# Attention scores on TensorE: one stacked query against paired key parts

## The chip, the cores and the metric

The kernel runs on one core of a Trainium2 chip. A core has five engines with a queue each: TensorE (PE in the profile; PEld is its weight load), VectorE (DVE), ScalarE (ACT), GpSimd (POOL) and SyncE (SP), which issues most DMAs here. Engines wait for each other through semaphores. The time is microseconds on the device for one execution. A matmul takes a stationary operand (loaded as weights, up to 128x128) and streams a moving operand of up to 512 columns past it; its result goes to PSUM, which DVE and ACT read.

## What is computed

The reference is one decoder block for 1024 positions and 1024 channels: a combined input projection, a spatial gating branch, a dilated window attention branch, a merge, and a convolutional MLP. The change is in the attention scores. There are three head groups with 4 heads of 64 dims each; a group with dilation `dil` splits the sequence into `dil` residues, and in each residue blocks of 128 queries see their own 128 keys and the 128 before them:

```python
DILATED_GROUPS = ((128, 1), (512, 4), (2048, 16))
def banded_window_attention(q, k, v, steps):
    ...
    qb = blocks(q)
    kc = with_prev(blocks(k))
    vc = with_prev(blocks(v))
    scores = jnp.einsum('nbqhd,nbkhd->nbhqk', qb, kc, ...) * (HEAD_DIM ** -0.5)
    ...
    band = (dist >= 0) & (dist <= steps)
    first_ok = (jnp.arange(nb)[:, None, None] > 0) | (ki[None] >= ATTN_BLOCK)
    scores = jnp.where(valid[None, :, None], scores, -jnp.inf)
    m = jnp.max(scores, axis=-1, keepdims=True)
    p = jnp.exp(scores - m)
    den = jnp.sum(p, axis=-1, keepdims=True)
    out = jnp.einsum('nbhqk,nbkhd->nbqhd', (p / den).astype(v.dtype), vc)
```

Everything is float32. The first block of a residue has no block before it, so it sees its own keys alone.

## The kernel before

**Numbers in two parts.** A float32 matmul would be slow on PE, so operands are split into a high part (rounded to `float32r`) and a low part (the rest, also `float32r`), and products are made of part products. `to_parts` makes them: ACT copies with rounding, DVE subtracts.

**Stages.** The input projection runs first, as 27 pairs of 128-column weight tiles; each pair is made by 7 products (a Strassen-like scheme, `in_product`, line 544), and each product is 12 matmuls of 128x512. From the pairs of group 1 on (order of the groups: 1, 2, 0), attention is woven into this stream. After every 6 projection matmuls `tick()` counts a clock on, and work that was put off with `after(lag, fn)` for that count is written out. So the order on PE is fixed by the program; on DVE, ACT, POOL and SP the order after the first 18 products is chosen by the framework's own planner when the program is built, and each engine then runs its queue strictly in that order.

**One block of attention** (class `Attend`, 24 of them: 8 for each group, `T` = 0 to 7) is started at tick `s` after its group's values are there: `load` brings the block's 64-dim queries and keys from DRAM, each twice, one copy in partitions 0 to 63 and one in 64 to 127 (line 840, SP; 3 buffers); `turn` at `s` makes the parts; `score` at `s+3` makes the scores (lines 865, 866), their maximum (line 879, DVE), and the exponentials (line 893, ACT, after the negated maximum on DVE, line 891); `turn_p` at `s+8` transposes them on PE (line 904) and copies the transposes out (910 ACT, 912 DVE); `product` at `s+10` multiplies by the values (line 920). Blocks start 5 ticks apart, so several are under way at once.

**The parts of a block.** `kk`, in a ring of 3 slots (`kring`), holds the keys' high part in partitions 0 to 63 and the low part in 64 to 127. `qa` and `qb` hold the high and the low part of the queries, each in both halves. A matmul of 128 partitions with `qa` thus sums query-high times key-high and query-high times key-low, and one with `qb` adds the two terms with query-low. So each head takes two matmuls of 256 columns, 8 per block.

**With and without a block before.** In group 0 blocks 1 to 7 have a block before them, in group 1 the odd ones, in group 2 none: 11 blocks have one, 13 have none. For the 11 the 256 columns are two ring slots. For the 13 the same 128 keys are streamed twice (a broadcast), and only columns 128 to 255 are used.

**Group 0** also mixes the three groups (`combine`, called in `product`): SP loads the stored results of groups 1 and 2 (line 939, tiles `ld`), DVE makes weights from them (lines 948 to 959), POOL applies them (971, 972). The first of these DVE instructions, `nmin` (line 948), waits for the loads; a load waits until POOL has finished with the same buffer one block earlier.

Of the kernel before, what the change touches and what calls it, by code (L numbers as in the profile page):

```python
# [12 lines left out]
F32R = mybir.dt.float32r  # L13
BF16 = mybir.dt.bfloat16
I32 = mybir.dt.int32
AF = mybir.ActivationFunctionType
ALU = mybir.AluOpType
# [3 lines left out]
P = 128  # L21
# [7 lines left out]
NH = 4  # L29
# [7 lines left out]
GROUPS = (1, 2, 0)  # L37
FIRST = 2
UW = NH * HD + 2 * NH
KSLOTS = 3  # L40

INV_FREQ = [float(np.float32(500000.0 ** (-i / ROT))) for i in range(0, ROT, 2)]

# [51 lines left out]
def block_kernel(  # L95
# [61 lines left out]
    def f32(ap):  # L157
        return ap.bitcast(F32)
# [654 lines left out]
    class Attend:  # L813
# [28 lines left out]
            self.q_raw, self.k_raw = got  # L842

        def turn(self):
            qa = at.tile([P, NH, P], F32R, name=f"qa_{self.name}", tag="qa", bufs=1)
            qb = at.tile([P, NH, P], F32R, name=f"qb_{self.name}", tag="qb", bufs=1)
            kk = kring[:, self.slot]
            nc.scalar.activation(kk, self.k_raw, AF.Copy)
            nc.vector.tensor_tensor(
                kk[64:P], self.k_raw[64:P], f32(kk[64:P]), ALU.subtract  # L850
            )
            to_parts(qa, qb, self.q_raw, nc.vector)
            self.qa, self.qb = qa, qb

        def score(self):
            name = self.name
            sc = ps_x.tile([P, 2, 2, 256], F32, name=f"sc_{name}", tag="sc")
            s0, s1 = (t % KSLOTS for t in self.halves)
            for h in range(NH):
                if self.has_prev:  # L860
                    keys = kring[:, s0 : s1 + 1 : s1 - s0, h, :]
                else:
                    keys = kring[:, s0, h, :].unsqueeze(1).to_broadcast([P, 2, P])
                dst = sc[:, h % 2, h // 2, :]
                nc.tensor.matmul(dst, self.qa[:, h, :], keys, start=True, stop=False)  # L865
                nc.tensor.matmul(dst, self.qb[:, h, :], keys, start=False, stop=True)  # L866
            lo = 0 if self.has_prev else P
            st = at.tile([P, UW], F32, name=f"st_{name}", tag="st", bufs=2)
            mx = small.tile([P, NH], F32, name=f"mx_{name}", tag="mx")
            pr_t = at.tile([P, NH, 256], F32, name=f"pr_{name}", tag="pr", bufs=2)  # L870
            if self.g == 2:
                mk = mask2
            elif self.has_prev:
                o = 0 if self.halves[0] < self.T else P
                mk = mask[:, o : o + 256]
            else:
                mk = mask[:, P : 2 * P]
            for h in range(NH):
                nc.vector.tensor_tensor_reduce(
                    out=pr_t[:, h, lo:256],  # L880
                    in0=sc[:, h % 2, h // 2, lo:256],
                    in1=mk,
                    op0=ALU.add,
                    op1=ALU.max,
                    scale=1.0,
                    scalar=-3.0e38,
                    accum_out=mx[:, h : h + 1],
                )
            nm = st[:, 256 : 256 + NH]
            den = st[:, 256 + NH : 256 + 2 * NH]  # L890
            nc.vector.tensor_scalar(nm, mx, -0.125, None, ALU.mult)
            for h in range(NH):
                nc.scalar.activation(
                    pr_t[:, h, lo:256], pr_t[:, h, lo:256], AF.Exp,
                    bias=nm[:, h : h + 1], scale=0.125, accum_out=den[:, h : h + 1],
                )
            self.st, self.pr = st, pr_t
# [115 lines left out]
    def open_attention():  # L1013


        nonlocal at, kring, mask, mask2
        at = at_stack.enter_context(tc.tile_pool(name="at", bufs=2, reuse_waits="tile"))
        kring = at.tile([P, KSLOTS, NH, P], F32R, name="kring", bufs=1)
        mask = at.tile([P, 3 * P], F32, name="mask", bufs=1)
        mask2 = at.tile([P, P], F32, name="mask2", bufs=1)  # L1020
        sign = at.tile([P, 256], F32, name="sign", tag="vt", bufs=8)[0:1, 0:P]
        nc.gpsimd.memset(mask, 0.0)
        nc.gpsimd.memset(sign[:, 0::2], 1.0)
        nc.gpsimd.memset(sign[:, 1::2], -1.0)
        for m in (mask[:, 0:P], mask[:, 2 * P : 3 * P]):
            nc.gpsimd.affine_select(
                out=m, in_=m, compare_op=ALU.is_ge, fill=NEG,
                base=0, pattern=[[1, P]], channel_multiplier=-1,
            )

        def causal(m):
            nc.gpsimd.affine_select(
                out=m, in_=m, compare_op=ALU.is_ge, fill=NEG,
                base=0, pattern=[[-1, P]], channel_multiplier=1,
            )

        def parity_mask():
            pg = tr_tile("pg")
            nc.tensor.matmul(pg[:, :P], sign, sign, start=True, stop=True)
            nc.vector.tensor_scalar(mask2, pg[:, :P], 1.0, -0.5 * NEG, ALU.subtract, ALU.mult)  # L1040
            causal(mask2)

        causal(mask[:, P : 2 * P])
        after(8, parity_mask)
# [1463 lines left out]
```

## Time and profile before

| what | value |
|---|---|
| three runs | 1362.97, 1362.97, 1362.02 us (median 1362.97) |
| the profiled execution's own time | 1362.35 us |
| its span in the profile | 1360.6 us (1.75 us lie around it) |
| granted TensorE clock | 0.998 |
| PE / DVE / ACT / POOL busy over the span | 1352.0 / 1030.4 / 642.0 / 313.5 us |
| score matmuls (lines 865, 866) | 192, from 157.4 to 391.6 us |
| stretch with attention in it, 150 to 401 us | PE 251.0 of 251 us busy, DVE 193.0, ACT 142.1 |

Rows of the timeline start with the start in us and the duration in us; then engine, line, operation, output <- input, how many were merged, and in brackets how long the engine was idle before and who ended that. Durations of PE's matmuls overlap (they are pipelined), so what one costs is the distance from one start to the next. DVE's instructions overlap a little in the same way: one of 0.68 us is followed by the next 0.60 us later. `L879` appears as a custom DVE instruction, with a short read of its accumulator behind it.

### The profile page before, as it was taken

The numbers are of one execution on the slowest core, as the hardware profiler recorded it, in microseconds if no ns is written. First come the engines' busy times: TensorE is split into PE (matmuls) and PEld (weight loads), VectorE is DVE, ScalarE is ACT, GpSimd is POOL, SyncE is SP. The second block draws the span as 40 slices with busy tenths as digits, with TensorE's granted clock in tenths as the row PEclk, the third lists the DMA queues.
The fourth block names the chain that finished last, engine by engine and source line by source line (L and its number), as shares of the span: only waits on it lengthen the run. The fifth ranks groups of instructions, "written<-read, shape, count | busy, mean of one in ns | idle before, by whom it ended". The sixth has DMA issues, their size and how long they took to land.

```text
span 1360.6 us, 19176 instructions
## 1 busy us (share of the span) xinstructions
PE 1352.0 (99%) x6408; PEld 1127.0 (83%) x6408; DVE 1030.4 (76%) x1881; ACT 642.0 (47%) x1269; POOL 313.5 (23%) x302
## 2 busy tenths in 40 slices
PE   9999999999999999999999999999999999999998
PEld 8888888888888888888888888888888888888886
DVE  7988686877877987769789878666666667686675
ACT  7662555556543335335456343333433335354453
POOL 1123000001330000220010336565655564000002
PEclk9999999999999999999999999999999999999999
DMA  9435453544438995884741133333233328986663
GB/s 354 112 93 179 134 168 103 153 152 129 136 112 286 311 318 181 289 272 149 254 157 54 58 103 105 106 117 102 100 109 124 121 85 291 377 314 229 202 207 124
DMA packets 144803, 237.01 MB, mean 174 GB/s; under 512 B 13888, under 2 KB 58432, under 8 KB 144704
## 3 DMA queue, kind: packets, MB, share of 16 engines
q1 hardware_dynamic: 142464, 231.79, 51.2%
q0 software_dynamic: 1088, 2.10, 0.9%
q10 hardware_dynamic: 1152, 1.89, 0.4%
q8 instruction: 51, 0.84, 0.3%
q14 instruction: 48, 0.39, 0.1%
HBM read 167.77 MB, written 64.29 MB: 171 GB/s over the span
## 4 chain that ended last, share of the span: by engine, by line
PE 97%; DVE 1%; SPq 1%; ACT 1%; POOL 0%; DMA 0%; issue 0%; POOLq 0%; DVEq 0%; ACTq 0%
PE in_P L544 28%; PE uP L1948 21%; PE dn L2211 15%; PE up L1948 8%; PE wo_P L1780 6%; PE pa L1410 5%; PE pl L617 3%; PE pu L920 2%; PE pu L1928 2%; PE pb L1410 2%; PE pp L904 1%; PE sc L865 1%; PE sc L866 1%; SPq L760 1%; PE pm L737 1%; PE ht L1684 1%
## 5 line engine op out<-in xcount | busy, mean ns | idle before, releaser
L544 PE MATMUL in_P<-R,G 128*128 128x512 f32 x1008 | 243.8, 394 | 0.0
L544 PEld LDWEIGHTS in_P<-R,G 128*128 128x128 f32 x1008 | 185.7, 188 | 37.0
L2211 PE MATMUL dn<-R 128*128 128x512 f32 x924 | 209.6, 389 | 0.0
L2211 PEld LDWEIGHTS dn<-R 128*128 128x128 f32 x924 | 173.5, 188 | 36.0
L312 ACT ACTIVATE G<-wr 128x512 fp32r<-128x512 f32 x126 | 78.9, 628 | 98.0 <-PE in_P L544 60.5
L170 ACT ACTIVATE R<-up 128x512 fp32r<-128x512 f32 x109 | 65.7, 623 | 123.3 <-DVE up L279 105.8
L544 PE MATMUL in_P<-G,G 128*128 128x512 f32 x504 | 122.8, 394 | 0.0
L1948 PE MATMUL uP<-G,R 128*128 128x512 f32 x504 | 121.4, 390 | 0.0
L1948 PE MATMUL uP<-R 128*128 128x512 f32 x504 | 121.2, 389 | 0.0
L1948 PE MATMUL up<-G,R 128*128 128x512 f32 x504 | 120.3, 389 | 0.0
L1948 PEld LDWEIGHTS uP<-G,R 128*128 128x128 f32 x504 | 94.4, 188 | 20.3 <-issue 0.4
L1948 PEld LDWEIGHTS up<-G,R 128*128 128x128 f32 x504 | 94.7, 188 | 19.7
L1948 PEld LDWEIGHTS uP<-R 128*128 128x128 f32 x504 | 94.6, 188 | 19.7
L544 PEld LDWEIGHTS in_P<-G,G 128*128 128x128 f32 x504 | 92.8, 188 | 19.2 <-issue 0.7
L313 DVE TENSOR_TENSOR G<-wr,G 128x512 fp32r<-128x512 f32 x126 | 88.1, 699 | 25.7 <-ACT G L312 24.7
L171 POOL TENSOR_TENSOR R<-up,R 128x512 fp32r<-128x512 f32 x55 | 73.1, 1342 | 13.2 <-ACT R L170 12.2
L170 ACT ACTIVATE R<-db 128x512 fp32r<-128x512 f32 x77 | 48.1, 626 | 53.8 <-PE dn L2211 43.6
L171 DVE TENSOR_TENSOR R<-db,R 128x512 fp32r<-128x512 f32 x77 | 52.6, 687 | 24.4 <-ACT R L170 24.3
L1410 PE MATMUL pa<-R,G 128*128 128x512 f32 x288 | 67.9, 389 | 0.0
L971 POOL TENSOR_TENSOR ld<-ld,w 128x256 f32<-128x256 f32 x16 | 11.3, 723 | 233.3 <-DVE w L959 233.3
L1410 PEld LDWEIGHTS pa<-R,G 128*128 128x128 f32 x288 | 54.1, 188 | 11.2
L544 PE MATMUL in_P<-G 128*128 128x512 f32 x252 | 61.9, 392 | 0.0
(300 smaller groups left out, 2475.4 us busy)
## 6 DMA issues: line engine op xcount, KB each, us to landing
up<-in_w_up_dram SPq DMA_DIRECT2D x44, 512.0 KB, 3.9
wr<-in_w_in_dram SPq DMA_DIRECT2D x42, 512.0 KB, 4.1
dA<-gd SPq DMA_DIRECT2D x55, 256.0 KB, 5.0
wd<-in_w_down_dram SPq DMA_DIRECT2D x44, 256.0 KB, 5.1
wT<-wd SPq DMA_DIRECT2D x44, 256.0 KB, 3.9
dS<-gS SPq DMA_DIRECT2D x44, 256.0 KB, 4.4
db<-wT SPq DMA_DIRECT2D x44, 256.0 KB, 4.6
gd<-Y SPq DMA_DIRECT2D x42, 256.0 KB, 2.0
```

Of the source, the lines that this page charges most:

```text
L170: nc.scalar.activation(hi, src, AF.Copy)
L171: fn = lambda: lo_eng.tensor_tensor(lo, src, f32(hi), ALU.subtract)
L312: lambda: nc.scalar.activation(op[:, 0], src, AF.Copy),
L313: lambda: nc.vector.tensor_tensor(op[:, 1], src, f32(op[:, 0]), ALU.subtract),
L544: nc.tensor.matmul(acc, op[:, w, kt, :], left[LEFT[name], kt][:, a, :], start=opened and i == 0, stop=i == len(HIGH_FIRST) - 1, skip_group ...
L617: nc.tensor.matmul(lead_banks[b][:, cs], raw_x[h, kt][:, a, c * P : (c + 1) * P], lead_op(kt, w, cs), start=kt == 0 and p == 0 and cs.star ...
L920: nc.tensor.matmul(pu[:, h * HD : (h + 1) * HD], self.pT[:, i, :], vt[:, h * HD : (h + 1) * HD], start=i % n == 0, stop=i % n == n - 1,)
L1410: nc.tensor.matmul(acc, unit[a][kt // 4][:, kt % 4, :], two(R, 8 * h + kt)[:, b, :], start=n == 0 and i == 0, stop=n == len(kts) - 1 and i ...
L1780: nc.tensor.matmul(acc, left[LEFT[name], kt][:, a, blk * P : (blk + 1) * P], out_ops[s][:, w, :], start=name not in SHARED and kt == 0 and ...
L1928: nc.tensor.matmul(acc, plain_up[which, k][:, w, kt, :], left[f"A{h + 1}{k + 1}", kt][:, a, :], start=n == 0 and i == 0, stop=n == KT - 1 ...
L1948: nc.tensor.matmul(acc, op[w][:, kt, :], left[LEFT[name], kt][:, a, :], start=opened and i == 0, stop=i == len(HIGH_FIRST) - 1, skip_group ...
L2211: nc.tensor.matmul(accs[blk], dops[s][:, 0, a, blk * P : (blk + 1) * P], dops[s][:, 1, w, :], start=SEQ[j] not in CONTINUES and kt == 0 an ...
```

## The change

Three edits in the two-part scores:

1. `turn`: the queries now take the stacked form, one tile `qs` with the high part in partitions 0 to 63 and the low part in 64 to 127. The keys take the paired form: the ring slot has a high and a low part, each in both halves. The ring has 2 slots instead of 3.
2. `score`, a block with one before it: still two matmuls per head, now with the same stationary `qs`, once against the high part of both slots, once against the low part.
3. `score`, a block with its own keys alone: one matmul per head; its 256 columns are 128 against the high part and 128 against the low part. The two results lie beside each other in PSUM and are summed on DVE: one new `tensor_tensor` for all 4 heads adds the mask to the low half and writes that into the unused columns 0 to 127 of `pr_t`; the maximum instruction then adds the high half to it, where it added the mask before.

```diff
-KSLOTS = 3
+KSLOTS = 2
...
-            qa = at.tile([P, NH, P], F32R, name=f"qa_{self.name}", tag="qa", bufs=1)
-            qb = at.tile([P, NH, P], F32R, name=f"qb_{self.name}", tag="qb", bufs=1)
-            kk = kring[:, self.slot]
-            nc.scalar.activation(kk, self.k_raw, AF.Copy)
+            qs = self.qs = at.tile([P, NH, P], F32R, name=f"qs_{self.name}", tag="qs", bufs=1)
+            nc.scalar.activation(qs, self.q_raw, AF.Copy)
             nc.vector.tensor_tensor(
-                kk[64:P], self.k_raw[64:P], f32(kk[64:P]), ALU.subtract
+                qs[64:P], self.q_raw[64:P], f32(qs[64:P]), ALU.subtract
             )
-            to_parts(qa, qb, self.q_raw, nc.vector)
-            self.qa, self.qb = qa, qb
+            to_parts(kring[:, self.slot, 0], kring[:, self.slot, 1], self.k_raw, nc.vector)
...
+                dst = sc[:, h % 2, h // 2, :]
                 if self.has_prev:
-                    keys = kring[:, s0 : s1 + 1 : s1 - s0, h, :]
+                    for part in range(2):
+                        keys = kring[:, s0 : s1 + 1 : s1 - s0, part, h, :]
+                        nc.tensor.matmul(
+                            dst, self.qs[:, h, :], keys, start=part == 0, stop=part == 1
+                        )
                 else:
-                    keys = kring[:, s0, h, :].unsqueeze(1).to_broadcast([P, 2, P])
-                dst = sc[:, h % 2, h // 2, :]
-                nc.tensor.matmul(dst, self.qa[:, h, :], keys, start=True, stop=False)
-                nc.tensor.matmul(dst, self.qb[:, h, :], keys, start=False, stop=True)
+                    nc.tensor.matmul(dst, self.qs[:, h, :], kring[:, s0, :, h, :], start=True, stop=True)
...
+            if not self.has_prev:
+                nc.vector.tensor_tensor(
+                    pr_t[:, :, 0:P].rearrange("p (b a) t -> p a b t", a=2), sc[:, :, :, P:256],
+                    mk.unsqueeze(1).unsqueeze(1).to_broadcast([P, 2, 2, P]), ALU.add,
+                )
             for h in range(NH):
                 nc.vector.tensor_tensor_reduce(
                     out=pr_t[:, h, lo:256],
-                    in0=sc[:, h % 2, h // 2, lo:256],
-                    in1=mk,
+                    in0=sc[:, h % 2, h // 2, 0 : 256 - lo],
+                    in1=mk if self.has_prev else pr_t[:, h, 0:P],
...
-        kring = at.tile([P, KSLOTS, NH, P], F32R, name="kring", bufs=1)
+        kring = at.tile([P, KSLOTS, 2, NH, P], F32R, name="kring", bufs=1)
```

Because the planner sets the queues of DVE, ACT and SP anew, the change also moves instructions that it does not touch. Three places, in the order of the built programs (line number, operation, output <- input, size; the line numbers of the changed program are 5 higher from line 880 on):

On PE, block T = 0 of group 1, first before and then after; `sc` is the score tile, `in_P` a projection bank, `avt` a transpose of values.

```order
L544 MATMUL in_P_1529<-R,G_76 128x512 x6
L865 MATMUL sc_0_1536<-kring,qa_0_1494 128x256
L866 MATMUL sc_0_1536<-kring,qb_0_1495 128x256
L865 MATMUL sc_0_1536<-kring,qa_0_1494 128x256
L866 MATMUL sc_0_1536<-kring,qb_0_1495 128x256
L865 MATMUL sc_0_1536<-kring,qa_0_1494 128x256
L866 MATMUL sc_0_1536<-kring,qb_0_1495 128x256
L865 MATMUL sc_0_1536<-kring,qa_0_1494 128x256
L866 MATMUL sc_0_1536<-kring,qb_0_1495 128x256
L1001 MATMUL avt_4_1557<-ident,C_103 128x128 x2
```

```order
L544 MATMUL in_P_1528<-R,G_76 128x512 x6
L866 MATMUL sc_0_1535<-kring,qs_0_1494 128x256 x4
L1006 MATMUL avt_4_1553<-ident,C_103 128x128 x2
```

Four matmuls stand where eight stood; nothing else moves on PE in the whole program.

On DVE, block T = 2 of group 1 (without a block before it), before and after; `st` is the negated maximum, `C` an eviction of a projection bank, and the rows `mx` alone, left out here, are the accumulator reads.

```order
L912 COPY pT_1_1727<-pp_1_4_1734 128x512
L879 ISA pr_2_1751,mx_2_1750<-sc_2_1740,mask 128x128
...
L171 TENSOR_TENSOR qb_3_1795<-q_3_1669,qa_3_1794 128x512
L891 TENSOR_SCALAR st_2_1749<-mx_2_1750 128x4
L574 TENSOR_TENSOR C_103<-C_103,in_P_1720 128x8x64
```

```order
L917 COPY pT_1_1721<-pp_1_4_1728 128x512
L879 TENSOR_TENSOR pr_2_1741<-sc_2_1734,mask 128x2x2x128
L848 TENSOR_TENSOR qs_3_1785<-q_3_1664,qs_3_1785 64x512
L884 ISA pr_2_1741,mx_2_1740<-sc_2_1734,pr_2_1741 128x128
...
L574 TENSOR_TENSOR C_103<-C_103,in_P_1714 128x8x64
L896 TENSOR_SCALAR st_2_1739<-mx_2_1740 128x4
```

The new add stands ahead of the four maxima, the query's low part too (it stood between them and `st`), and an eviction now stands ahead of `st`.

On DVE, group 0, block T = 4 (it has a block before it), before and after; `nmin_3694` and `nmin_3634` are the mixing of block 3, and wait for its `ld` tiles.

```order
L912 COPY pT_3_3621<-pp_3_4_3628 128x512
L879 ISA pr_4_3645,mx_4_3644<-sc_4_3634,mask 128x256
...
L587 TENSOR_TENSOR C_103<-C_103,in_P_3525 128x512
L313 TENSOR_TENSOR G_76<-wt_14_3591,G_76 128x512
L948 TENSOR_TENSOR nmin_3694<-ld_3_3689,ld_3_3691 128x4
L171 TENSOR_TENSOR qb_5_3716<-q_5_3532,qa_5_3715 128x512
L949 TENSOR_TENSOR nmin_3694<-nmin_3694,st_3_3510 128x4
L849 TENSOR_TENSOR kring<-k_6_3664,kring 64x512
L891 TENSOR_SCALAR st_4_3643<-mx_4_3644 128x4
```

```order
L917 COPY pT_3_3561<-pp_3_4_3568 128x512
L953 TENSOR_TENSOR nmin_3634<-ld_3_3629,ld_3_3631 128x4
L884 ISA pr_4_3585,mx_4_3584<-sc_4_3574,mask 128x256
...
L587 TENSOR_TENSOR C_103<-C_103,in_P_3466 128x512
L313 TENSOR_TENSOR G_76<-wt_14_3531,G_76 128x512
L954 TENSOR_TENSOR nmin_3634<-nmin_3634,st_3_3451 128x4
L848 TENSOR_TENSOR qs_5_3655<-q_5_3473,qs_5_3655 64x512
...
L171 TENSOR_TENSOR kring<-k_5_3476,kring 128x512
L896 TENSOR_SCALAR st_4_3583<-mx_4_3584 128x4
```

The mixing's first instruction now stands ahead of the block's maxima, and the keys' low part written here is that of block 5, where it was that of block 6.

## The prediction

> **What bounds the kernel now.** I read the page's busy times first, then its chain, then the waits of PE.
>
> ```profile
> PE 1352.0 (99%) x6408; PEld 1127.0 (83%) x6408; DVE 1030.4 (76%) x1881; ACT 642.0 (47%) x1269; POOL 313.5 (23%) x302
> PE 97%; DVE 1%; SPq 1%; ACT 1%; POOL 0%; DMA 0%; issue 0%; POOLq 0%; DVEq 0%; ACTq 0%
> PE warm L395 <- POOL ident masks.py:199: 1.7, 1, 1.7
> PE pm L733 <- DVE C L740: 0.2, 1, 0.2
> ```
>
> PE is busy for 99% of the span and carries 97% of the chain that ends last. The last two rows are its whole list of waits: 1.9 us in all. So what leaves PE's queue shortens the program, as long as no engine that feeds PE becomes late; and since PE waits for nothing now, the change can remove no wait, only add some. Whether the feeders have room is read by stage. These three stretches are those of groups 1, 2 and 0 (columns: length, then busy time of PE, PEld, DVE, ACT, POOL, granted clock, DMA share, GB/s):
>
> ```profile
> 150.00:240.00 90.00, 90.00 (x508) 77.30 (x506) 66.73 (x159) 52.16 (x135) 0.00 (x0) 1.00 0.45 133
> 240.00:318.00 78.00, 78.00 (x431) 66.81 (x431) 57.30 (x151) 44.68 (x123) 0.00 (x0) 1.00 0.49 144
> 318.00:401.00 83.00, 83.00 (x491) 72.37 (x491) 68.97 (x230) 45.24 (x125) 22.22 (x28) 1.00 0.40 124
> ```
>
> PE has no gap in any of them. DVE is at 74%, 73% and 83%, ACT at 58%, 57% and 55%.
>
> **The change part by part.** *Score matmuls.* They are these, at these distances (the block T = 0 of group 1, first and last of its eight, and what follows):
>
> ```profile
> L865 PE MATMUL sc<-kring,qa x96: 278/283/364, 157.4 to 391.5; 128*128 128x256 f32 x96
> 157.44 0.28 PE L865 MATMUL sc<-kring,qa 128*128 128x256 f32 x1
> 158.28 0.28 PE L866 MATMUL sc<-kring,qb 128*128 128x256 f32 x1
> 158.40 0.27 PE L1001 MATMUL avt<-ident,C 128*128 128x128 f32 x1
> ```
>
> The duration of 283 ns is not the price, since they overlap. Eight take 158.40 − 157.44 = 0.96 us, so one costs 0.12 us. There are 96 on line 865 and as many on 866; 13 of the 24 blocks drop four each, 52 matmuls: 52 × 0.12 = **6.2 us** off PE's queue. The 11 other blocks keep eight of the same size. For the new order of operands there (one stationary tile used twice, another moving pattern) the nearest row is the same one, so I count no difference.
>
> The Trainium skill, TensorE: Matmul & The Clock Gate, section "Part 2: What happens when you issue a matmul", gives 262 cycles at 2.4 GHz for one matmul of 256 columns behind another, 109 ns; by that estimate the gain would be 5.7 us. The row above, 0.12 us, decides.
>
> *Parts of queries and keys.* ACT rounds two tiles of 512 columns per block before and after. DVE makes two low parts per block, one of 64 and one of 128 partitions; only which is which changes. No cost in itself.
>
> *The new add.* 13 on DVE. The nearest rows are an add that also reads a PSUM bank and SBUF (line 579), and the same size held up by POOL's traffic (797):
>
> ```profile
> L579 DVE TENSOR_TENSOR C<-C,in_P 128x512 f32<-128x512 f32 x10 | 6.8, 683 | 3.4 <-PE in_P L544 3.4
> L797 DVE TENSOR_TENSOR C<-C,YC 128x512 f32<-128x512 f32 x4 | 3.6, 912 | 0.0
> ```
>
> So between 0.68 and 0.91 us each; I take 0.68, since it reads PSUM as line 579 does: 13 × 0.68 = 8.9 us more on DVE, spread over the 13 blocks. It is off PE's path unless PE reaches the transposes of the block before its exponentials are done. In these blocks the order on DVE puts three things of 0.6 us ahead of the negated maximum that were not there: the add, the query's low part, an eviction: 1.8 us later. What PE has in hand (T = 0 of group 1, then T = 1 of group 2: the negated maximum, the last piece of the exponentials, the transposes on PE):
>
> ```profile
> 160.27 0.16 DVE L891 TENSOR_SCALAR st<-mx 128x4 f32<-128x4 f32 x1
> 160.85 1.28 ACT L893 ACT_TABLE_LOAD   x1
> 163.61 0.19 ACT L893 ACTIVATION_READ_ACCUMULATOR pr<-pr,st 128x1 f32 x1
> 166.22 0.60 PE L904 MATMUL pp<-ident,pr 128*128 128x128 f32 x4
> 253.16 0.17 DVE L891 TENSOR_SCALAR st<-mx 128x4 f32<-128x4 f32 x1
> 254.82 0.19 ACT L893 ACTIVATION_READ_ACCUMULATOR pr<-pr,st 128x1 f32 x1
> 258.60 0.60 PE L904 MATMUL pp<-ident,pr 128*128 128x128 f32 x4
> ```
>
> In T = 0 there are 166.22 − 163.80 = 2.4 us, and the table load in front of the exponentials starts 0.4 us after the negated maximum is there, so up to 0.4 + 1.3 us of delay cost nothing. In T = 1 of group 2 there are 3.6 us. PE arrives 0.5 us earlier (four matmuls fewer), so 1.8 + 0.5 = 2.3 us are to be covered: covered in both, barely in the first without the table load. Cost on the path: 0.
>
> *Two slots in place of three.* In groups 0 and 1 the keys' parts of block T + 1 now go into the slot that the scores of T − 1 and T read, so they are written after the scores of T, as the queries' parts already were; `qs` and `kring` of T + 1 then stand one behind the other on ACT and DVE. Of the SP queue, key loads now follow the queries' low part and query loads the keys' (the buffers come free in that order); several query and key loads and weight loads change places. The weights are loaded 9 products ahead, and PE shows no wait for a load. No cost, as long as DVE writes both parts before the next scores.
>
> *Group 0, T = 4.* Here the planner's new order can reach PE. Before (the transposes' copy, first maximum, mixing, negated maximum, last piece of the exponentials, PE's eight transposes, next scores):
>
> ```profile
> 360.00 0.68 DVE L912 COPY pT<-pp 128x512 f32<-128x512 f32 x1
> 360.60 0.41 DVE L879 CUSTOM_DVE_ANT_0 pr<-sc,mask 128x256 f32<-128x256 f32 x1
> 363.42 0.16 DVE L948 TENSOR_TENSOR nmin<-ld,ld 128x4 f32<-128x4 f32 x1 [0.17 <-DMA ld<-scr]
> 365.04 0.17 DVE L891 TENSOR_SCALAR st<-mx 128x4 f32<-128x4 f32 x1
> 367.14 0.19 ACT L893 ACTIVATION_READ_ACCUMULATOR pr<-pr,st 128x1 f32 x1
> 368.51 1.04 PE L904 MATMUL pp<-ident,pr 128*128 128x128 f32 x8
> 369.31 0.36 PE L865 MATMUL sc<-kring,qa 128*128 128x256 f32 x1
> ```
>
> The mixing (363.42) waited for its load until then. After the change it stands ahead of the first maximum, so DVE stands still from 360.60 until the load lands. That is 363.4 again, or 362.8, since one low part (0.6 us) moved behind the previous block's mixing, which lets POOL and the next load start sooner. From there the maxima and two more take 363.42 − 0.17 − 360.60 = 2.65 us, the rest to the negated maximum 365.04 − 363.42 = 1.62 us and 0.2 us for three small ones that moved ahead: 362.8 + 0.1 + 2.65 + 1.8 = 367.35, so 2.3 us late. The exponentials end at 367.33 + 2.3 = 369.6. PE needs the last head's at the seventh transpose, 368.51 + 6 × 0.10 = 369.1. A wait of **0.5 us**; with the load at 363.4, 1.1 us. What is late next is this block's mixing, by about 1 us, and with it the load that T = 5 waits for. T = 5 and T = 6 before:
>
> ```profile
> 378.83 0.19 ACT L893 ACTIVATION_READ_ACCUMULATOR pr<-pr,st 128x1 f32 x1
> 379.17 1.04 PE L904 MATMUL pp<-ident,pr 128*128 128x128 f32 x8
> 389.21 0.19 ACT L893 ACTIVATION_READ_ACCUMULATOR pr<-pr,st 128x1 f32 x1
> 389.87 1.04 PE L904 MATMUL pp<-ident,pr 128*128 128x128 f32 x8
> ```
>
> To the seventh transpose T = 5 has 379.77 − 379.02 = 0.75 us and T = 6 has 390.47 − 389.40 = 1.07 us. T = 5 is late by 1 us less the 0.5 us that PE itself lost: covered. In T = 6 the keys' low part (0.6 us) moves ahead of the negated maximum: covered, if nothing else is late. I add 0.1 us for the two.
>
> **Sum.** −6.2 + 0.5 + 0.1 = **−5.6 us**. Against the profiled execution: 1362.35 − 5.6 = 1356.75. The median of the runs is 0.62 us above that execution, so **1357.4 us**. Bounds of the unknown: the waits lie between 0 (6.2 us gained, 1356.8) and 3 us (T = 4 at 1.1, T = 5 and 6 at 0.9 each when every delay adds up: 1359.8).
>
> **The rivals.** *Half of it goes to group 0.* Seven blocks there have a block before them and little in hand (to PE's arrival 379.17 − 379.02 = 0.15 us in T = 5 and 0.47 us in T = 6). If each lost the 0.6 us of one DVE instruction, 4.2 us would come back: −2.0 us, 1361.0, no measurable change. For it: DVE at 83% there. Against: in five of the seven (all but T = 4 and 6) as many DVE instructions stand ahead of the negated maximum as before.
>
> *DVE becomes the bound (slower).* If the new add lay on PE's path in all 13 blocks, 13 × 0.68 = 8.9 us would meet 6.2 us: +2.7 us, 1365.7. It decides once the delay per block passes what PE has in hand, 3.6 us in group 2, that is, once DVE falls behind by two more instructions than the order says. Against: 57.30 of 78 us busy in that stage, 62 with eight adds, and projection operands that the program makes up to four products ahead.
>
> *The matmuls cost more than their distance.* If a weight load did not lie beside the matmul before it, a pair would cost its 0.19 us more and 52 pairs 16 us: 1347. The eight pairs in 0.96 us say no. The Trainium skill, same page, "Part 3: Packing small matmuls", says that a weight load overlaps matmuls in flight only where the row groups differ; the trace (190 ns loads, 120 ns distance, all on 128 rows) disagrees.
>
> **How the numbers follow.** A measurement of this kernel tells about 0.2% (2.7 us) from no change, so faster means below 1360.2. The forecast, with waits up to 3 us: 0.80. Waits of 3.5 us and more, up to no gain (the first rival): 0.13, of which I put 0.01 in the faster. DVE as bound: 0.06. Dearer matmuls: 0.01. Faster 0.82, same 0.12, slower 0.06. The likeliest case's own range is 1356.2 to 1359.8, with 0.6 us of spread between the runs below. The range goes further up, into the first rival: 1355.9 to 1361.0; outside lie the slower case, the dearer matmuls and a few hundredths more.
>
> **What the changed profile would show.** 140 score matmuls in place of 192, still 0.12 us apart, and four between the neighbours in a block with its own keys. The new add on DVE at 0.68 us, 13 times. PE's list of waits: nothing in groups 1 and 2; under 1.5 us in group 0, at the transposes of T = 4 to 6, ended by the exponentials. DVE idle ahead of the mixing in T = 4 by about 2 us, ended by a load. Wrong would be the forecast if PE waits for exponentials in blocks without a block before them, if scores wait for `kring`, or if projection matmuls wait for DVE.

## The result, and the profile after

The changed kernel takes 1358.28 us (median of 8 runs, 1357.27 to 1359.83) against 1363.08 us for the kernel before (8 runs beside it). The ratio is 0.9967, with a 95% interval of 0.9958 to 0.9977: 4.8 us less, and faster by more than the 0.2% that a measurement can tell. The forecast was 1357.4 us. The profiled execution took 1359.83 us, the longest of the eight; its span is 1358.1 us, against 1360.6 before.

From the page of the kernel after, busy times and chain, and three of the new rows in its list of waits of PE (us in total, times, longest):

```profile
PE 1346.1 (99%) x6356; PEld 1118.8 (82%) x6356; DVE 1034.8 (76%) x1894; ACT 641.7 (47%) x1269; POOL 311.8 (23%) x302
PE 89%; DMA 3%; DVE 3%; ACT 1%; POOL 1%; SPq 1%; issue 1%; POOLq 0%; DVEq 0%; ACTq 0%
PE rs_bc L427 <- DVE YC L421: 0.9, 1, 0.9
PE in_P L544 <- DVE C L579: 0.8, 1, 0.8
PE in_P L544 <- DVE C L581: 0.3, 1, 0.3
```

PE has 52 instructions less and is busy for 5.9 us less, DVE has 13 more and is busy for 4.4 us more. PE now waits where it did not: at `rs_bc` (line 427, the row norms at the very start) and for evictions of a projection bank (lines 579 and 581); two more new waits are of 0.5 and 0.2 us. None of these places is one that the change edits. The three stretches, groups 1, 2 and 0:

```profile
150.00:240.00 90.00, 90.00 (x502) 76.98 (x500) 70.11 (x165) 52.46 (x134) 0.00 (x0) 1.00 0.46 137
240.00:318.00 78.00, 78.00 (x422) 66.31 (x421) 63.96 (x170) 46.06 (x127) 0.00 (x0) 1.00 0.52 154
318.00:401.00 83.00, 82.89 (x484) 71.62 (x484) 67.88 (x223) 44.01 (x123) 22.39 (x28) 1.00 0.40 119
```

DVE went from 67 to 70 us in group 1 and from 57 to 64 us in group 2. PE is still without a gap in both. In group 0 it has one now, of 0.1 us by this count. The parts of the change itself, by line, and the block T = 0 of group 1 on PE:

```profile
L866 PE MATMUL sc<-kring,qs x52: 278/282/364, 159.3 to 315.0; 128*128 128x256 f32 x52
L879 DVE TENSOR_TENSOR pr<-sc,mask x13: 680/685/692, 160.0 to 315.3; 128x512 f32<-128x512 f32 x13
159.26 0.64 PE L866 MATMUL sc<-kring,qs 128*128 128x256 f32 x4
159.73 0.38 PE L1006 MATMUL avt<-ident,C 128*128 128x128 f32 x2
```

Four matmuls in 159.73 − 159.26 = 0.47 us, 0.12 us each, where eight took 0.96 us. The add takes 0.68 us, as forecast.

To find where the time went I use one distance on PE: from the first scores (group 1, T = 0) to those of the last block (group 0, T = 7). All 13 blocks with their own keys alone lie between. Before, the last block's first score matmul and that of T = 6 are these:

```profile
379.96 0.36 PE L865 MATMUL sc<-kring,qa 128*128 128x256 f32 x1
390.66 0.36 PE L865 MATMUL sc<-kring,qa 128*128 128x256 f32 x1
```

So before it is 390.66 − 157.44 = 233.22 us; after, 386.92 − 159.26 = 227.66 us (the row of 386.92 stands below). That is 5.56 us gained, of 13 × 0.48 = 6.24 that the matmuls give: 0.7 us are missing. The rest of the way is no better than before: the first scores came 1.8 us later in this execution, and from the last block's scores to the next stage PE lost 0.9 us. That makes three questions: what ate 0.7 us between the scores; whether the new add has a part in it; and whether the two losses outside belong to the change.

The 0.7 us stand in group 0. From the scores of T = 4 to those of T = 5 it took 10.70 us before and takes 10.76 after; from T = 6 to T = 7 it took 10.70 and takes 11.30. All other distances in group 0 are as before within 0.02 us from T = 1 on. First T = 6 before (the issue of the load of the other groups' results; the mixing's first instruction, which waits for it; the negated maximum):

```profile
379.84 1.48 SPq L939 DMA_DIRECT2D ld<-scr  x2
383.10 0.16 DVE L948 TENSOR_TENSOR nmin<-ld,ld 128x4 f32<-128x4 f32 x1 [0.98 <-DMA ld<-scr]
387.11 0.17 DVE L891 TENSOR_SCALAR st<-mx 128x4 f32<-128x4 f32 x1
```

And after (also the two low parts, the last piece of the exponentials, the transposes, the next scores):

```profile
375.62 1.20 PE L862 MATMUL sc<-kring,qs 128*128 128x256 f32 x8
375.96 1.47 SPq L944 DMA_DIRECT2D ld<-scr  x2
379.66 0.16 DVE L953 TENSOR_TENSOR nmin<-ld,ld 128x4 f32<-128x4 f32 x1 [1.43 <-DMA ld<-scr]
382.85 0.69 DVE L848 TENSOR_TENSOR qs<-q,qs 64x512 fp32r<-64x512 f32 x1
383.79 0.68 DVE L171 TENSOR_TENSOR kring<-k,kring 128x512 fp32r<-128x512 f32 x1
384.40 0.16 DVE L896 TENSOR_SCALAR st<-mx 128x4 f32<-128x4 f32 x1
386.49 0.18 ACT L898 ACTIVATION_READ_ACCUMULATOR pr<-pr,st 128x1 f32 x1
385.52 1.64 PE L909 MATMUL pp<-ident,pr 128*128 128x128 f32 x8
386.92 1.20 PE L862 MATMUL sc<-kring,qs 128*128 128x256 f32 x8
```

Counted from this block's scores (379.96 before, 375.62 after), `nmin` comes at 4.04 us in place of 3.14, and the negated maximum at 8.78 in place of 7.15: 1.63 us later. Of that, 0.46 us is a later issue of the load, 0.44 us a longer way of it, and the other 0.73 us is the keys' low part (line 171), which now also stands ahead of the negated maximum. PE had 1.07 us in hand; its transposes take 1.64 us in place of 1.04, and the next scores come 0.60 us late. The list of waits above does not hold this wait: it is spread over eight transposes, whose time counts as busy. The load's longer way is seen in the list of DMA issues around it (KB each, median us to landing), first before, then after:

```profile
ld<-scr SPq DMA_DIRECT2D x2, 132.0 KB, 2.0
```

```profile
ld<-scr SPq DMA_DIRECT2D x2, 132.0 KB, 2.9
k<-kd SPq DMA_DIRECT2D x2, 128.0 KB, 3.1
```

A load of keys was issued in the same 10 us after, and none before. That it is what makes the load of the results longer is likely, but no run shows it.

At T = 4 the stall that the forecast priced at 0.5 us is there, but smaller:

```profile
356.30 0.68 DVE L917 COPY pT<-pp 128x512 f32<-128x512 f32 x1
358.04 0.16 DVE L953 TENSOR_TENSOR nmin<-ld,ld 128x4 f32<-128x4 f32 x1 [1.06 <-DMA ld<-scr]
364.53 0.19 ACT L898 ACTIVATION_READ_ACCUMULATOR pr<-pr,st 128x1 f32 x1
364.10 1.10 PE L909 MATMUL pp<-ident,pr 128*128 128x128 f32 x8
```

DVE stood still for 1.06 us, not the 2.2 us that the forecast reckoned with (362.8 − 360.60). The exponentials end at 364.72, and the eight transposes take 1.10 us in place of 1.04.

### The profile page after: what moved, and what is told of

Same layout as the page of the kernel before. It is cut to its first block, busy times and chain, and to the rows that moved or that the text cites. A ratio compares the mean times of both kernels' runs of the same rounds, so it can differ in the third digit from the quotient of the medians.

```text
span 1358.1 us, 19080 instructions
## 1 busy us (share of the span) xinstructions
PE 1346.1 (99%) x6356; PEld 1118.8 (82%) x6356; DVE 1034.8 (76%) x1894; ACT 641.7 (47%) x1269; POOL 311.8 (23%) x302
## 4 chain that ended last, share of the span: by engine, by line
PE 89%; DMA 3%; DVE 3%; ACT 1%; POOL 1%; SPq 1%; issue 1%; POOLq 0%; DVEq 0%; ACTq 0%
PE in_P L544 24%; PE uP L1953 21%; PE dn L2216 15%; PE up L1953 8%; PE wo_P L1785 6%; PE pa L1415 5%; PE pu L925 2%; PE pu L1933 2%; PE pb L1415 2%; PE pl L617 1%; PE pp L909 1%; SPq L760 1%; DMA ld<-scr 1%; DMA YC<-in_x_dram 1%; POOL st L977 1%
```

## The experiments

Theory: the matmuls give 13 × 0.48 = 6.24 us; the add is hidden; 0.7 to 0.8 us are lost in group 0 through the planner's new order, and nothing else belongs to the change. Rivals: the add (DVE) takes a part of the gain; the late start and the wait for line 579 belong to the new layout.

**The changed kernel again.** No edit.

> The changed kernel as it is, a second profile. My theory: 1357.5 to 1359 us; 227.0 to 228.2 us from the first scores of group 1 to the last block's scores in group 0 (233.3 before, 227.7 in the first profile after); the 0.6 us lost around T=6 of group 0 is there again, because the order of the instructions makes it. Rival: the late start (1.8 us by the first scores) and the 0.8 us wait for the later stage's products at about 485 us belong to the change too; then both are here again, with the same size. If they are of that one execution, the start is back within 0.5 us of the kernel before and the wait under 0.3 us.

1358.89 us (5 runs, ratio 0.9967, 0.9954 to 0.9979); 385.91 − 158.11 = 227.80 us. The loss in group 0 is there again (0.28 us at T = 4, 0.53 at T = 6). The start is 0.7 us late and the wait for line 579 is 0.6 us: both smaller than in the first profile, neither gone. That left them open.

**The new layout alone**, two passes per head and no add:

```diff
-                    nc.tensor.matmul(dst, self.qs[:, h, :], kring[:, s0, :, h, :], start=True, stop=True)
+                    for part in range(2):
+                        keys = kring[:, s0, part, h, :].unsqueeze(1).to_broadcast([P, 2, P])
+                        nc.tensor.matmul(
+                            dst, self.qs[:, h, :], keys, start=part == 0, stop=part == 1
+                        )
...
-            if not self.has_prev:
-                nc.vector.tensor_tensor(...)
```

> The new layout of queries and keys alone: a block with its own keys alone keeps two passes of 256 columns per head (eight matmuls, the query's parts one after the other), and has no add on VectorE. My theory: the layout itself costs nothing, so the time is that of the kernel before within 0.6 us (1362.4 to 1363.7), with 233 us between the first scores and the last block's. Rival: the layout's other copies and their order, not the add, lose the 0.6 us in group 0 that was seen after; then it is 0.5 us and more above the kernel before.

1363.98 us (11 runs, ratio 1.0003, 0.9994 to 1.0013). By time alone that is no clear difference. By the distance it is the rival that came true:

```profile
158.77 1.11 PE L868 MATMUL sc<-kring,qs 128*128 128x256 f32 x8
391.22 1.57 PE L908 MATMUL pp<-ident,pr 128*128 128x128 f32 x8
392.55 1.19 PE L862 MATMUL sc<-kring,qs 128*128 128x256 f32 x8
```

392.55 − 158.77 = 233.78 us, 0.56 more than before, nearly all of it (0.54) at the transposes of T = 6, which took 1.57 us. The loss in group 0 needs neither the add nor an earlier PE; it comes with the layout and the order that the planner makes of it.

**Four matmuls in the layout of before**, no add:

```diff
-                nc.tensor.matmul(dst, self.qa[:, h, :], keys, start=True, stop=False)
-                nc.tensor.matmul(dst, self.qb[:, h, :], keys, start=False, stop=True)
+                nc.tensor.matmul(dst, self.qa[:, h, :], keys, start=True, stop=not self.has_prev)
+                if self.has_prev:
+                    nc.tensor.matmul(dst, self.qb[:, h, :], keys, start=False, stop=True)
```

> The layout of before, but the blocks with their own keys alone leave out the matmul with the query's low part: four instead of eight matmuls, no add. The scores of those 13 blocks lack the terms of the query's low part. My theory: 13 x 0.48 = 6.2 us less than before, 1356.8 us, within 0.4 us, since the matmuls' price is simply 0.12 us each and nothing waits more. Rival: the gain of the PE is capped by the exponentials and copies behind it also without the add; then it is 5.6 us or less, as in the changed kernel, and PE waits at T=6 of group 0 here too.

1356.38 us (5 runs, ratio 0.9953, 0.9941 to 0.9966). The distance is 384.53 − 157.54 = 226.99 us, 6.23 less than before, and no transposes in group 0 wait. The matmuls' price is confirmed to 0.01 us, and with the old order of DVE the earlier PE alone makes no wait.

**Two passes of 128 columns per head**, summed in PSUM, no add, in the new layout:

```diff
-                    nc.tensor.matmul(dst, self.qs[:, h, :], kring[:, s0, :, h, :], start=True, stop=True)
+                    for part in range(2):
+                        nc.tensor.matmul(
+                            dst[:, P:256], self.qs[:, h, :], kring[:, s0, part, h, :],
+                            start=part == 0, stop=part == 1,
+                        )
```

> The changed kernel's layout, but the blocks with their own keys alone take the sum over the keys' parts in PSUM: two matmuls of 128 columns per head, the second accumulating, and no add on VectorE. My theory: a matmul of 128 columns costs nearly what one of 256 does here (0.12 us for 256; the lower bound by columns is 0.06, the upper 0.12 and, if these fp32 columns are streamed slower when fewer stand in one instruction, up to 0.24). By 0.06 the time is that of the changed kernel less what the add cost, 1357.6 or so; by 0.12 it is that of the kernel before, 1363; by 0.24 it is 13 x 0.96 = 12.5 us above that, 1375.5. I expect 0.12 or more, so no less than 1363.

1362.39 us (11 runs, ratio 0.9996, 0.9988 to 1.0005): as before the change, and a little below the 1363 that was expected. The block T = 0 of group 1:

```profile
157.44 1.00 PE L867 MATMUL sc<-kring,qs 128*128 128x128 f32 x8
158.28 0.41 PE L1005 MATMUL avt<-ident,C 128*128 128x128 f32 x2
```

Eight of 128 columns take 0.84 us where eight of 256 took 0.96: half the columns for 0.105 us in place of 0.12, where 0.12 or more was expected. (The distance, 390.13 − 157.44 = 232.69 us, says the same: 0.53 us less than before although 0.49 us are lost in group 0, so 1.02 us for 104 matmuls, 0.01 each.) What the change saves is the number of matmuls, hardly their columns; to put both parts beside each other in one matmul was the point of it.

**The kernel before again.** No edit.

> The kernel before as it is, a second profile. It tells which differences in the profiles are of one execution. In the seven profiles so far the first scores of group 1 start between 157.4 and 159.3 us, and the wait of the projections for C at 469 to 485 us is 0 to 1.5 us. My theory: both come from loads, differ from execution to execution, and the start lies anywhere in that range here; from the first scores to the last block's in group 0 it is 233.2 us within 0.2, as in the first profile. Rival: they belong to the new layout; then the start is 157.5 within 0.2 and there is no wait at 469 to 485 us.

One run, 1361.58 us. 390.63 − 157.41 = 233.22 us to the hundredth, the start as in the first profile, and no wait for line 579: for once on the side of the rival, that start and wait belong to the layout. Later profiles speak against it: the changed kernel's third has no such wait, and with five adds (the same program up to the first scores) these come at 157.84 us.

**The copies one tick earlier** (in the changed kernel, so that the planner makes another order):

```diff
-            after(s, self.turn)
+            after(max(1, s - 1), self.turn)
```

> The changed kernel, but the copies of a block's queries and keys are written out one tick (6 projection matmuls) earlier. The planner then puts nmin of group 0 behind the maxima at T = 4, and at T = 6 it puts both subtractions of the copies and the negated maximum ahead of nmin, which waits for the load of the other groups' results. My theory: the 0.6 to 0.8 us lost in group 0 come from that order alone, so from the first scores to the last block's it is 227.0 us as without any add and with the order of before (227.7 and 227.8 in the changed kernel), and the time is 0.7 us less, 1357.5 to 1358.2. Rival: they come from the load itself, which the new layout's other loads delay; then nothing is gained here, 227.7 us again.

1355.60 us (5 runs, 1355.37 to 1356.12; ratio 0.9947, 0.9934 to 0.9959). Group 0, T = 6, and the last scores (the negated maximum, `nmin`, the last piece of the exponentials, the transposes):

```profile
379.45 0.17 DVE L896 TENSOR_SCALAR st<-mx 128x4 f32<-128x4 f32 x1 [0.47 <-issue]
379.56 0.16 DVE L953 TENSOR_TENSOR nmin<-ld,ld 128x4 f32<-128x4 f32 x1
381.55 0.19 ACT L898 ACTIVATION_READ_ACCUMULATOR pr<-pr,st 128x1 f32 x1
383.35 1.04 PE L909 MATMUL pp<-ident,pr 128*128 128x128 f32 x8
384.14 1.19 PE L862 MATMUL sc<-kring,qs 128*128 128x256 f32 x8
```

With the negated maximum ahead of `nmin`, the exponentials end 1.6 us before the transposes begin. The distance is 384.14 − 157.15 = 226.99 us, the same as with four matmuls in the old layout without any add. So the add costs PE nothing, and the whole loss in group 0 goes with the order. The time is 0.8 us less for that. It is 2.7 to 3.3 us less than the changed kernel's, below the range that was expected, so there must be a second reason.

**The mixing one tick later**, behind the loads it needs:

```diff
             others.append(t)
+            after(1, lambda: self.mix(pu, others))
...
-            after(5, self.turn_y)
+            after(4, self.turn_y)
```

> The changed kernel, but in group 0 the mixing of the three groups is written out one tick after the loads of the other groups' results instead of together with them. The planner then puts maxima, both subtractions and the negated maximum ahead of nmin at T = 4 and T = 6. My theory: no wait of PE at the transposes in group 0, 227.0 us from the first scores to the last block's, 1357.5 to 1358.2. Rival: the mixed output comes a tick later than before, the next block's products pu wait for the bank that the mixing reads; then PE waits at pu instead, and it is 227.7 us or more.

1355.84 us (5 runs, ratio 0.9959, 0.9945 to 0.9972); 384.13 − 157.15 = 226.98 us. The same gain on PE by another way to nearly the same order (the negated maximum ahead of `nmin`), and no new wait at the products. The time is below the expected range here too.

**The add made five times** (for the later ones the same with two and three):

```diff
-            if not self.has_prev:
+            for _ in range(0 if self.has_prev else 5):
                 nc.vector.tensor_tensor(...)
```

> The changed kernel, but the add in front of the maxima is made five times in each block with its own keys alone (the same result each time). Each takes 0.60 us from start to start, so 2.4 us more per block, 31 us in all on DVE. DVE is busy 64 of the 78 us of group 2 now, with 8 such blocks: 83 of 78 with the repeats. My theory that the one add is hidden because DVE has room: here the room is used up, PE waits at the transposes of group 2, and the time rises by 4 to 12 us above the changed kernel's, to 1362 to 1370. If the add were on the path already (the rival in which DVE is the bound), it would rise by the whole 13 x 2.4 = 31 us, to 1390.

1390.85 us (4 runs, ratio 1.0206, 1.0190 to 1.0221): 32.6 us above the changed kernel, which is the rival's number (31) and far outside the 4 to 12 us that were expected. By the number alone one would say that DVE is the bound and each add costs its 0.60 us. The profile says something else. One block of group 2 on DVE (first and last add, first maximum), then PE's waits in the stretch, three pieces of 3.41 us in a row, and a fourth from later (the columns as above):

```profile
266.06 0.69 DVE L879 TENSOR_TENSOR pr<-sc,mask 128x512 f32<-128x512 f32 x1 [0.79 <-PE sc L866]
271.64 0.68 DVE L879 TENSOR_TENSOR pr<-sc,mask 128x512 f32<-128x512 f32 x1
272.84 0.28 DVE L884 CUSTOM_DVE_ANT_0 pr<-sc,pr 128x128 f32<-128x128 f32 x1
```

```profile
PE pp L909 <- ACT pr L898: 13.4, 11, 2.6
261.85:265.26 3.41, 2.07 (x10) 1.03 (x9) 3.38 (x8) 2.17 (x9) 0.00 (x0) 1.00 0.24 52
265.26:268.68 3.42, 3.42 (x12) 2.84 (x11) 2.53 (x5) 1.23 (x2) 0.00 (x0) 0.50 0.68 179
268.68:272.09 3.41, 3.41 (x20) 2.94 (x20) 2.22 (x5) 1.15 (x2) 0.00 (x0) 1.00 0.19 52
326.70:330.11 3.41, 2.25 (x11) 1.55 (x9) 3.23 (x13) 1.26 (x5) 0.00 (x0) 1.00 0.12 42
```

The planner puts another DVE instruction (or a stall) behind each add, so the maxima start 6.8 us after the first add. With one add it was 1.4 us (276.01 to 277.43 in the changed kernel's block at 275 us). A delay of 5.4 us meets 1.6 us in hand in the tightest block (in the changed kernel the exponentials end at 273.3 us there, and its transposes begin at 274.9): PE waits 13.4 us in 11 places, and after six of them the granted clock falls to 0.50 for 3.41 us, as in the second of the four pieces. The distance from the first scores to the last block's is 420.94 − 157.84 = 263.10 us, 35.3 more than in the changed kernel (227.81). The half clock is worth some 10 of them (an estimate, 6 × 3.41 × 0.5), the listed waits 13.4; and 13 × 0.83 = 10.8 are transposes, whose four in a block lie 1.16 us from first to last start where it was 0.33, which the list does not count. DVE itself was busy for 130.6 of the 158 us from 160 to 318 us, so it was not full. So the rival's 31 was met by chance, for other reasons. The next two show it.

**The add made twice, and three times**, on the kernel with the copies one tick earlier:

> The kernel with the copies one tick earlier, but the add is made twice in each block with its own keys alone (the same result). The planner puts one other instruction of DVE behind each add, as it does behind the one that is there, so that a further add delays the maxima by about 0.60 + 0.65 = 1.25 us. The smallest slack of a block with its own keys alone, from the end of the exponentials to the first transpose, was 1.7 us in the changed kernel's profile. My theory (the add is hidden up to that slack): 1.7 - 1.25 = 0.4 us are left, no wait, 227.0 us from the first scores to the last block's, and the time stays within 1 us of the kernel with the copies one tick earlier, about 1356. Rival (DVE is already the bound): 13 x 0.6 = 8 us more, 1363 and above.

1356.81 us (4 runs, ratio 0.9953, 0.9938 to 0.9968), 384.50 − 157.51 = 226.99 us: 13 more adds, 8 us of DVE, cost PE nothing between the scores. By the whole time it is 0.8 to 1.2 us more than with one add, of which this distance shows nothing.

> As the kernel with one more add, but with the add made three times in each block with its own keys alone. My theory: 1.7 - 2.5 = -0.8 us, so the transposes of the tightest blocks now wait for the exponentials, most of all in group 2; 13 blocks at up to 0.8 us each are up to 10 us, 1357 to 1367, with waits of PE ended by the exponentials in groups 1 and 2. If the four repeats' 33 us came from the sum of the adds alone, it would be 13 x 1.2 = 16 us, 1371.

1359.10 us (10 runs, ratio 0.9970, 0.9961 to 0.9979), 385.45 − 156.62 = 228.83 us: 1.84 us more, in two blocks of the 13. The larger of the two:

```profile
281.86 1.48 PE L909 MATMUL pp<-ident,pr 128*128 128x128 f32 x4 [0.44 <-ACT pr L898]
```

In this distance 0, 1.8 and 35.3 us for one, two and four more adds (the last on the changed kernel): a threshold, not a price per add. Of the up to 10 us that were expected 1.8 came, since eleven blocks still had room, and the two that waited are not the tightest. With one add this block (T = 4 of group 2) has 2.8 us in hand, the tightest 1.9. With three adds the planner put its first add 2.9 us behind its scores (275.83 against 272.95), where it was 0.8. So the order of the queue decides here too.

**The changed kernel and the one with earlier copies, side by side.** No further edit.

> The changed kernel a third time, on the same chip as the next one. My theory: again a wait of 0.6 us or more in group 0 (227.7 us) and one of 0.5 to 1.5 us for C at about 485 us; 1358.3 to 1359. Rival: the wait at 485 us is chance and gone.

1357.88 us (5 runs, ratio 0.9961, 0.9948 to 0.9973); 386.31 − 158.50 = 227.81 us, the loss in group 0 for the third time (0.12 us at T = 4, 0.69 at T = 6). The wait for line 579 is not there: the rival was right.

> The kernel with the copies one tick earlier a second time, beside the changed kernel on one chip. My theory: 227.0 us, no wait at 485 us, and 1.3 to 3 us less than the changed kernel. Rival: the 2.7 us between the two in the earlier runs was mostly the chips' difference; then it is less than 0.8 us.

1356.06 us (6 runs, ratio 0.9952, 0.9939 to 0.9965); 384.59 − 157.60 = 226.99 us; 1.8 us less than the changed kernel beside it, as the theory had it (1.3 to 3). Of it 0.8 is group 0; the other 1.0 lies outside the scores, and its cause isn't shown.

**The losses outside.** The wait for line 579 lies in the stage behind attention, where DVE also works on the loaded `w_down` tiles (columns: busy, mean ns of one, idle time ahead of them and what ended it). First the changed kernel in its first and its third profile:

```profile
L1076 DVE TENSOR_TENSOR wd<-wd,wd 128x512 f32<-128x512 f32 x37 | 25.3, 688 | 7.9 <-DMA wd<-in_w_down_dram 7.4
```

```profile
L1076 DVE TENSOR_TENSOR wd<-wd,wd 128x512 f32<-128x512 f32 x39 | 26.7, 688 | 5.7 <-DMA wd<-in_w_down_dram 5.2
```

Then the kernel with two passes of 128 columns:

```profile
L1075 DVE TENSOR_TENSOR wd<-wd,wd 128x512 f32<-128x512 f32 x34 | 23.2, 688 | 8.4 <-DMA wd<-in_w_down_dram 8.0
PE in_P L544 <- DVE C L579: 1.5, 1, 1.5
```

DVE waited 7.4 us for these loads where PE then waited 0.8 us, 5.2 where it waited none, 8.0 where it waited 1.5. The loads differ from execution to execution of one kernel, and in the other profiles too the wait of PE goes with them, but loosely: none at 6.3 us (before), 0.7 at 6.1 (the layout alone). That the loads cause it is argued, not shown. Nor is it shown that the new layout has no part: the three profiles of the old one have 0, 0 and 0.2 us for line 579, the eleven of the new one 0 to 1.5. The late start is another matter. In the profiles of before, of the four matmuls alone, and of the kernels with earlier copies or later mixing, the first scores come at 156.6 to 157.6 us, with two passes of 128 columns at 157.4, with the layout alone at 158.8; in all three profiles of the changed kernel at 158.1 to 159.3, and PE waits 0.5 to 0.9 us at `rs_bc`. Yet the changed kernel and the one with earlier copies have the same instructions in the same order on PE throughout, and on DVE, ACT and SP well into group 1. The changed kernel with five adds is the same program on every engine up to the first scores; these came at 157.84 us there, without a wait at `rs_bc`. So it is not the order; what it is stays open.

## Why the prediction was right

The distances say it in one table (us; the gain is against 233.22):

| kernel | matmuls, own keys | adds | order in group 0 | distance | gain | ratio of times |
|---|---|---|---|---|---|---|
| before, twice | 8 | 0 | old | 233.22, 233.22 | 0 | 1 |
| layout alone | 8 | 0 | new | 233.78 | −0.56 | 1.0003 |
| 128 columns | 8 | 0 | new | 232.69 | 0.53 | 0.9996 |
| four matmuls alone | 4 | 0 | old | 226.99 | 6.23 | 0.9953 |
| changed, three times | 4 | 1 | new | 227.66, 227.80, 227.81 | 5.41 to 5.56 | 0.9961 to 0.9967 |
| copies earlier, twice | 4 | 1 | mended | 226.99, 226.99 | 6.23 | 0.9947, 0.9952 |
| mixing later | 4 | 1 | mended | 226.98 | 6.24 | 0.9959 |
| one more add | 4 | 2 | mended | 226.99 | 6.23 | 0.9953 |
| two more adds | 4 | 3 | mended | 228.83 | 4.39 | 0.9970 |
| four more adds | 4 | 5 | new | 263.10 | −29.88 | 1.0206 |

- *Score matmuls, −6.2 us.* Right: 6.23 us. That eight of 256 columns with the other operands keep their distance was right too. The 5.7 us by the figure of the Trainium skill (TensorE: Matmul & The Clock Gate, "Part 2: What happens when you issue a matmul") were too low: 52 matmuls at 0.12 us, not 0.109.
- *The new add, 0.68 us, no cost.* Right in size and in effect: 226.99 us with it and without it. The rival that DVE becomes the bound fell; PE begins to wait for the adds between two and three per block, measured on the kernel with earlier copies. One row was read wrongly on the way: line 797 was said to be held up by POOL's traffic, but two of its four instructions took 1.11 and 1.17 us at 175.4 and 182.0 us, where POOL runs nothing (0.00 in the stretches of groups 1 and 2). What holds them up isn't shown; the 0.91 us was only the upper bound for the add.
- *Two slots, "no cost".* Not quite. In the new layout the keys' parts are written after the scores, and in T = 6 this puts 0.7 us more ahead of the negated maximum. No run has the new layout with three slots, so the slots' own part isn't shown.
- *Group 0, T = 4, 0.5 us.* The mechanism was right, the size was not: 0.06, 0.28 and 0.12 us. Counted from the block's scores (358.61 before, 354.20 after), the copy ahead of the stall came at 2.10 us instead of 1.39, since one more instruction of line 313 (0.7 to 0.9 us) now stands just ahead of it, and the load let `nmin` go at 3.84 us where 4.19 were reckoned. So DVE stood still for 1.06 us instead of 2.2.
- *T = 5 and 6, 0.1 us.* This is the step that failed: "covered, if nothing else is late" for T = 6. Something else was late, the load that `nmin` waits for, by 0.9 us, and with the keys' low part that is 1.63 us against 1.07 in hand. T = 6 lost 0.53 to 0.69 us. Order and load are both needed: with five adds the order in T = 6 is the new one too, but the load was issued 1.11 us ahead of the block's scores, `nmin` came at 2.63 us behind them, and T = 6 lost nothing. The waits together are 0.7 to 0.8 us for a forecast 0.6: nearly the right sum from two wrong parts, which is luck.
- *The remaining 0.9 us* between 1357.4 and 1358.28: at most 0.2 of them lie between the scores (5.41 to 5.56 us gained there for a forecast 5.6), and 0.1 is the kernel before, whose median was 1363.08 beside the changed one. The rest lies outside: the late start and, in two of three profiles, the wait for line 579. The prediction had taken the same times as before for both. That projection matmuls wait for DVE was one of its signs of being wrong; the sign came, some 100 us behind the last scores, and whether the change has a part in it stays open.

The rival that half the gain goes to group 0 was wrong: two of its seven blocks lost time, 0.8 us at most in all, not 4.2.

## What to carry to other kernels

When a framework plans the queues, an edit moves instructions in blocks that it does not touch; look there for what stands ahead of a wait, and try the same edit written out a tick earlier or later. Here that alone gave the whole 6.2 us between the scores, and a kernel that beats both (1355.6 and 1356.1 us). Work added to an engine with room is free as long as the delay stays within each block's slack, and can then cost more than its own length (from three adds to five, 15.6 us of DVE, some 34 us of the distance, between kernels that also differ by the 0.8 us of group 0). So read each block's slack, and the delay that the queue's order makes of the work there, rather than the engine's share of busy time.

## What the runs showed of the hardware

- *Half the columns, nearly the same price.* A matmul of 128 columns cost 0.105 us in the stream and one of 256 columns 0.12 us. The Trainium skill, TensorE: Matmul & The Clock Gate, "Part 2: What happens when you issue a matmul", gives about 81 ns for 128 columns in a stream with weight loads; the measured 105 ns is dearer than that.
- *A short wait can halve the clock, and where it falls decides.* With five adds the granted clock fell to 0.50 six times, each time for 3.41 us: at 169.69, 193.58, 237.96, 265.26, 309.63 and 357.42 us. From one fall to the next it is 7, 13, 8, 13 and 14 times 3.41 us, so the falls lie on a fixed grid. In the six slots of this grid just ahead of them PE was busy for 0.71, 1.85, 2.07, 2.07, 2.09 and 2.13 of the 3.41 us; in the four next lowest slots, which no fall followed, for 2.25 to 2.55. So a wait of 1.16 us at 262.6 us, with four slow transposes behind it in the same slot, halved the clock, and one of 1.16 us at 328.9 us, at the end of its slot, did not; nor did one of 1.39 us at 285.0 us, which two slots share. This is one run; where between 2.13 and 2.25 us the limit lies, and whether transposes count like other matmuls, it can't tell. The Trainium skill, TensorE: Matmul & The Clock Gate, "Part 1: The HAM clock gate", speaks of an idle window of about 3.4 us; the trace agrees with the length, but PE did not have to be idle for all of it.
